# A decay chain and a normalisation with operands in PSUM, and a later place for six weight-column reductions

## The chip, the cores and the metric

One core of a Trainium2 chip runs the whole layer. Five engines work beside each other: TensorE (PE, matrix products), VectorE (DVE), ScalarE (ACT), GpSimd (POOL) and SyncE (SP, which issues nearly all DMAs). The metric is the device time of one execution in microseconds; lower is better.

## The reference

One layer of a decoder trunk on `x` of 1024 tokens by 1024 features, float32. A conditioning vector gives six modulation vectors of 1024 values (`silu(c) @ w_ada + b_ada`). The first half of the layer:

```python
h = rms_norm(x, norm1_w) * (1.0 + scale1) + shift1
proj = h @ w_in            # gq gk gv gz (512 each), ga gb (8 each), sq (512), sk sv (128 each)
q_g, k_g = l2_norm(silu(conv(gq))), l2_norm(silu(conv(gk)))
beta = sigmoid(gb)
g = -exp(a_log) * softplus(ga + dt_bias)       # log-decay, one number per token and head
o_g = gated_delta_rule_chunked(q_g, k_g, v_g, g, beta)   # chunks of 64 tokens, G = cumsum(g) in a chunk
o_s = sliding_window_attention(sq, sk, sv)     # window 128
x = x + gate1 * (concat(o_g, o_s) @ w_out)
```

The second half is a SwiGLU feed-forward network on a second modulated norm. It is not touched here.

## The kernel before

Features lie on the 128 partitions, tokens on the free axis, in two halves of 512 tokens. Each float32 product is made of three: a high part `hi`, rounded by ACT, and a low part `lo = value - hi` stand for both operands, and `mm3` (L223) issues hi*hi, hi*lo, lo*hi. One "step" is one such triple for one block of 128 features; a projection unit of 128 columns by 512 tokens is eight steps into one PSUM bank.

The text of the kernel is traced by a framework. PE runs its instructions in the order in which they are written. On the other engines, and in the DMA queue of SP, a planner sets a fixed order from its own simulated times and from priorities: `tc.high_priority()` raises what is traced in it, and `tc.issue_after(ins)` places what is traced in it behind `ins`, but only those instructions that run on the engine of `ins`. All engines then run their queues in order and wait for semaphores.

Four PSUM banks (tags `u`, `sw`, two buffers each) serve the projection units, four more (tags `q0`, `q1`, and two of `qq`) everything else; `sm()` hands out these in turn.

The work around the change, in order:

- A start stage (to about 66 us) normalises the first half of the tokens and runs the first four projection units and three units of the small projection (`skv`: keys and values of the window attention, `ga`, `gb`).
- The second half of norm 1: `norm1_gen(1, 3)` squares, sums, takes the root, and `rstd_row` (L295) spreads it over the partitions by four transposes into the bank `rowps`, which ACT copies to `row` in SBUF. `modulate1` (L352) then makes `hi` and `lo` for each of the eight feature blocks: even blocks by a product on DVE (L343), ACT's rounding (L344), and a low part on DVE (L345); odd blocks by a product on POOL (L346), two passes on ACT (L348, L349), and a low part on DVE (L350).
- The adaptation columns: each of 48 columns needs the row products of a 128x1024 weight tile, loaded by SP (L260), with a broadcast of the conditioning vector. DVE does it in one instruction (L266), POOL in two products and ACT in a sum (L269, L270). `ada_pair` gives one column to POOL and one to DVE. Columns 0 to 15 are in the start stage, 16 to 31 (eight pairs) are queued behind the norm, 32 to 43 (six pairs) come later, 44 to 47 still later.
- `fill(n)` issues `n` steps of the dense stream: the units gk2, gq2 (both halves), skv 4 to 7, and then, from step 67, the units gk0, gq0, gk1, gq1 (second half), gk3, gq3 and so on. Each finished unit is evacuated by a causal convolution: ACT's first tap (L376), three DVE taps from PSUM (L378), three short DVE corrections from `tails` (L384), and ACT's Silu.
- `token_gen` (L656): the decay chain. For 128x64 numbers (8 heads by 8 blocks of 128 tokens) it makes beta and g with 21 small DVE instructions and three exponentials on ACT (L661 to L681), all on the SBUF tile `tsc`; then the sums over a chunk on PE (`psg`, L686) with DVE's copies of them (L688, L689) and ACT's exponentials (L690 to L692); then transposes (`pst`, L697) and stores to the DRAM tile R, which every pair reads back.
- `PAIRS` (L898): for each of four pairs of heads three visits (`pair_stats`, `pair_rows`, `pair_products`), each between two `fill` calls of the list `VISITS_A`. Then a triangular `solve` (L827) on DVE, the scan over chunks, the window attention, the output projection and the feed-forward network.

In the kernel before, 66 steps of the dense stream stand ahead of the chain, 22 between the chain and its sums, 4 between sums and transposes, and 4 more before the first pair's visit.

Of the kernel before, what the change touches and what calls it, by code (L numbers as in the profile page):

```python
# [12 lines left out]
AF = mybir.ActivationFunctionType  # L13
# [4 lines left out]
P = 128  # L18
# [4 lines left out]
H = 8  # L23
# [31 lines left out]
def tile_hybrid_layer(  # L55
# [61 lines left out]
    def r(ap):  # L117
        return ap.bitcast(F32R)
# [35 lines left out]
    def xs(k, hf):  # L154
        return xt[k // 2, hf][:, k % 2]
# [39 lines left out]
    def pool_tt(out, in0, in1, op, n):  # L195

        m = out.shape[1] // n
        for i in range(n):
            s_ = slice(i * m, (i + 1) * m)
            done["pool"] = pool.tensor_tensor(out=out[:, s_], in0=in0[:, s_], in1=in1[:, s_], op=op)  # L200
# [94 lines left out]
    def rstd_row(rs, name, q=None):  # L295

        pr = sm(f"rowps_{name}", q)
        for i in range(4):
            pe.transpose(out=pr[:, i * P:(i + 1) * P], in_=bc(rs[:, i:i + 1], (P, P)), identity=ident)
        row = t2(f"row_{name}")  # L300
        done["row"] = act.activation(out=row, in_=pr, func=AF.Copy)
        return row

# [35 lines left out]

    def modulate(hi, lo, out, x, row, a, sh, eng):  # L340

        if eng is dve:
            done["dve"] = dve.scalar_tensor_tensor(out=out, in0=x, scalar=a, in1=row, op0=ALU.mult, op1=ALU.mult)  # L343
            act.activation(out=r(hi), in_=out, func=AF.Identity, bias=sh)  # L344
            done["lo"] = dve.scalar_tensor_tensor(out=r(lo), in0=out, scalar=sh, in1=hi, op0=ALU.add, op1=ALU.subtract)  # L345
        else:  # L346
            pool_tt(out, x, row, ALU.mult, 1)
            act.activation(out=r(hi), in_=out, func=AF.Identity, scale=a, bias=sh)  # L348
            act.activation(out=out, in_=out, func=AF.Identity, scale=a, bias=sh)  # L349
            done["lo"] = dve.tensor_tensor(out=r(lo), in0=out, in1=hi, op=ALU.subtract)  # L350

    def modulate1(k, hf, row):  # L352
        hi, lo = h_hl(hf)(k)
        modulate(hi, lo, xs(k, hf), xs(k, hf), row, a1[:, k:k + 1], modc[:, k:k + 1], dve if (k % 2 == 0 if hf else k in (0, 1, 2, 7)) else pool)

# [275 lines left out]
    next(n1)  # L631
    for k in range(KT):
        modulate1(k, 1, rows[1])
    h_done = done["pool"], done["lo"]
    for u in (2, 3):
        EVAC[START[u][0]](START[u][1], 0, ps_u[u])
    for i in range(3):
        skv_out(ps_s[i], i)

# [16 lines left out]
    def token_gen():  # L656
        tsc = t4("tsc", (P, 16, H, NB), tag="a")
        xa, eb, ab, ue, ss_, s2, lp, gt = (tsc[:, n] for n in range(8))
        ealog = tsc[:, 8, :, 0]
# [11 lines left out]
        dve.tensor_scalar(out=ss_, in0=ue, scalar1=2.0, scalar2=None, op0=ALU.add)  # L671
        dve.reciprocal(out=ss_, in_=ss_)
        dve.tensor_tensor(out=ss_, in0=ss_, in1=ue, op=ALU.mult)
        dve.tensor_tensor(out=s2, in0=ss_, in1=ss_, op=ALU.mult)
        dve.tensor_scalar(out=lp, in0=s2, scalar1=1.0 / 17.0, scalar2=None, op0=ALU.mult)
        for n in (15, 13, 11, 9, 7, 5, 3):
            dve.scalar_tensor_tensor(out=lp, in0=lp, scalar=1.0 / n, in1=s2, op0=ALU.add, op1=ALU.mult)
        dve.scalar_tensor_tensor(out=lp, in0=lp, scalar=1.0, in1=ss_, op0=ALU.add, op1=ALU.mult)
        dve.tensor_scalar(out=xa, in0=xa, scalar1=0.0, scalar2=None, op0=ALU.max)
        dve.scalar_tensor_tensor(out=lp, in0=lp, scalar=2.0, in1=xa, op0=ALU.mult, op1=ALU.add)  # L680
        done["token"] = dve.scalar_tensor_tensor(out=gt, in0=lp, scalar=-1.0, in1=bc(ealog.unsqueeze(2), (P, H, NB)),  # L681
                                                 op0=ALU.mult, op1=ALU.mult)
# [5 lines left out]
        dve.tensor_copy(out=gst[:, 2], in_=psg[:, 0:64])  # L688
        dve.tensor_tensor(out=ed.rearrange("p h b -> p (h b)"), in0=psg[:, 64:128], in1=gst[:, 2], op=ALU.subtract)  # L689
        act.activation(out=gst[:, 3], in_=psg[:, 64:128], func=AF.Exp)  # L690
        act.activation(out=gst[:, 1], in_=gst[:, 2], func=AF.Exp)
        act.activation(out=ed, in_=ed, func=AF.Exp)  # L692
        dve.tensor_scalar(out=gst[:, 0], in0=beta.rearrange("p h b -> p (h b)"), scalar1=-1.0, scalar2=None, op0=ALU.mult)
        yield
# [224 lines left out]
    for i in range(11):  # L919
        fill(VISITS_A[0])  # L920
        if i < ADA_FIRST:
            with tc.issue_after(h_done[0].ins), tc.issue_after(h_done[1].ins):
                ada_pair()
    with tc.high_priority():
        next(token)

    with tc.issue_after(done["token"].ins):
        for i in range(11, 14):
            fill(VISITS_A[0])
            for _ in range(3):  # L930
                if ada_next[0] < 44:
                    ada_pair()
    p0, p1, p2, p3 = PAIRS
    for n, visit in zip(VISITS_A[1:], (token, token, p2, p0, p2, p0, p2, p1, p0, keys, p1, p3, keys, p1, keys, p3, p3)):
        fill(n)
        with tc.high_priority():
            next(visit)
# [770 lines left out]
```

## Time and profile before

| | |
|---|---|
| median of 3 runs | 1285.83 us (1284.82 to 1289.03) |
| profiled execution, its own time | 1288.89 us |
| its span, first to last instruction | 1287.2 us |
| PE busy | 1192.2 us (93%) |
| DVE busy | 855.9 us (66%) |
| ACT busy | 534.5 us (42%) |
| POOL busy | 525.9 us (41%) |
| mean granted PE clock | 0.959 of full speed |

Busy times are of one profiled execution. A busy time holds any slowing that the instruction met while it ran, so an instruction of one form can have two very different lengths. Idle time of an engine is listed with what ended it.

### The profile page before, as it was taken

The page shows a single profiled execution, that of the slowest core. Times are in us where ns is not written, and L with a number is a line of the kernel's source. Part 1 is how long each engine was busy: PE and PEld are TensorE (multiplying, and loading weights), DVE is VectorE, ACT ScalarE, POOL GpSimd, SP SyncE. Part 2 cuts the span into 40 slices and gives each one's busy share as a digit, 9 for nine tenths or more (in the row PEclk, how much of TensorE's full clock was granted, in tenths as well). Part 3 has the DMA queues.
Part 4 walks back from the last instruction along what each step waited for, and adds up shares of the span by engine and source line. Part 5 has one row for each costly group of instructions (what it writes and reads, how often), then busy time and mean ns, then how long its engine had stood idle before and what let it go on. Part 6 is the DMA issues. An engine that isn't in the chain of part 4 may idle for free.

```text
span 1287.2 us, 18639 instructions
## 1 busy us (share of the span) xinstructions
PE 1192.2 (93%) x6710; PEld 980.0 (76%) x6710; DVE 855.9 (66%) x1487; ACT 534.5 (42%) x973; POOL 525.9 (41%) x434
## 2 busy tenths in 40 slices
PE   6869497997999899999997989999999999999998
PEld 5758376885788677788876868888888888788887
DVE  6988989879323577545656469777888786665420
ACT  4374455522334587434554442222222243544430
POOL 4677455647536344365544420000000025366440
PEclk8899799997999799999999989999999999999999
DMA  8638369594749756343486885565455678776651
GB/s 331 229 99 310 115 126 241 169 259 130 208 147 213 105 98 154 126 147 134 170 263 219 289 271 192 185 223 172 157 174 176 238 248 307 273 268 202 212 164 41
DMA packets 173548, 250.61 MB, mean 195 GB/s; under 512 B 41360, under 2 KB 107152, under 8 KB 171920
## 3 DMA queue, kind: packets, MB, share of 16 engines
q1 hardware_dynamic: 163856, 241.03, 58.6%
q0 software_dynamic: 9600, 8.39, 4.4%
q8 instruction: 53, 0.87, 0.3%
q14 instruction: 39, 0.32, 0.1%
HBM read 182.89 MB, written 66.45 MB: 194 GB/s over the span
## 4 chain that ended last, share of the span: by engine, by line
PE 61%; DVE 19%; DMA 10%; ACT 5%; issue 2%; SPq 2%; POOL 1%; DVEq 0%; ACTq 0%; POOLq 0%
PE ps_S L1404 7%; PE ps_S L1402 7%; PE ps_S L1403 7%; PE ps_P L1403 5%; PE ps_P L1402 5%; PE ps_P L1404 5%; PE ps_o L225 2%; PE ps_o L227 2%; PE ps_o L226 2%; PE ps_c L1402 2%; PE ps_c L1403 2%; PE ps_c L1404 2%; DVE ada L458 1%; DMA rP<-in_wdown_dram 1%; DMA sd<-in_wdown_dram 1%
## 5 line engine op out<-in xcount | busy, mean ns | idle before, releaser
L200 POOL TENSOR_TENSOR wP<-rP,wP 128x512 fp32r<-128x512 f32 (+1 forms) x84 | 110.1, 1324 | 394.7 <-ACT wP L204 393.3
L1403 PE MATMUL ps_P<-t,wP 128*128 128x512 f32 x308 | 120.5, 391 | 1.1 <-DVE t L208 1.1
L1402 PE MATMUL ps_P<-t,wP 128*128 128x512 f32 x308 | 120.7, 392 | 0.1
L1404 PE MATMUL ps_P<-t,wP 128*128 128x512 f32 x308 | 120.4, 391 | 0.0
L204 ACT ACTIVATE wP<-rP 128x512 fp32r<-128x512 f32 (+1 forms) x84 | 47.4, 588 | 76.9 <-PE ps_P L1404 31.7
L1402 PE MATMUL ps_c<-B,w 128*128 128x512 f32 x176 | 70.3, 400 | 9.1 <-ACT X L1446 9.0
L1403 PE MATMUL ps_c<-B,w 128*128 128x512 f32 x176 | 69.5, 395 | 0.0
L1404 PE MATMUL ps_c<-B,w 128*128 128x512 f32 x176 | 69.5, 395 | 0.0
L1403 PEld LDWEIGHTS ps_P<-t,wP 128*128 128x128 f32 x308 | 57.8, 188 | 14.5 <-DVE t L208 2.2
L1402 PEld LDWEIGHTS ps_P<-t,wP 128*128 128x128 f32 x308 | 57.8, 188 | 12.9 <-ACT t L204 0.5
L1404 PEld LDWEIGHTS ps_P<-t,wP 128*128 128x128 f32 x308 | 57.8, 188 | 12.7
L200 POOL TENSOR_TENSOR ada<-ada,cb 128x512 f32<-128x512 f32 x34 | 50.5, 1517 | 19.1 <-DMA w_gz_0r<-in_wmain_dram 10.7
L1512 ACT ACTIVATE sg<-sg 128x512 f32<-128x512 f32 x33 | 20.9, 632 | 88.0 <-DVE sg L1508 88.0
L225 PE MATMUL ps_o<-mix,w_o 128*128 128x512 f32 x128 | 51.8, 405 | 0.0
L227 PE MATMUL ps_o<-mix,w_o 128*128 128x512 f32 x128 | 50.0, 391 | 0.0
L226 PE MATMUL ps_o<-mix,w_o 128*128 128x512 f32 x128 | 50.0, 391 | 0.0
L1589 DVE SCALAR_TENSOR_TENSOR x1r<-ps_P,modc,x1r 128x512 f32<-128x512 f32 x16 | 11.9, 747 | 54.6 <-PE ps_P L1404 54.6
L1402 PEld LDWEIGHTS ps_c<-B,w 128*128 128x128 f32 x176 | 33.7, 192 | 18.1 <-ACT X L1446 11.2
L1402 PE MATMUL ps_S<-T,wS2h 128*128 128x512 f32 x88 | 35.6, 404 | 3.9 <-ACT wS2h L204 3.9
L1404 PEld LDWEIGHTS ps_c<-B,w 128*128 128x128 f32 x176 | 33.6, 191 | 7.2
L1403 PEld LDWEIGHTS ps_c<-B,w 128*128 128x128 f32 x176 | 33.6, 191 | 6.8
L1404 PE MATMUL ps_S<-T,wS2l 128*128 128x512 f32 x88 | 35.6, 404 | 1.0 <-DVE wS2l L208 1.0
(500 smaller groups left out, 3644.0 us busy)
## 6 DMA issues: line engine op xcount, KB each, us to landing
ada<-in_ada_dram SPq DMA_DIRECT2D x48, 512.0 KB, 4.8
AD<-ops SPq DMA_DIRECT2D x11, 1536.0 KB, 6.1
w<-in_wgate_dram SPq DMA_DIRECT2D x44, 256.0 KB, 3.1
w<-in_wup_dram SPq DMA_DIRECT2D x44, 256.0 KB, 3.8
rP<-SD SPq DMA_DIRECT2D x16, 704.0 KB, 5.5
sd<-in_wdown_dram SPq DMA_DIRECT2D x20, 512.0 KB, 5.6
SD<-sd SPq DMA_DIRECT2D x20, 512.0 KB, 3.6
rP<-in_wdown_dram SPq DMA_DIRECT2D x12, 704.0 KB, 5.7
```

Source lines behind the costliest of these rows:

```text
L200: done["pool"] = pool.tensor_tensor(out=out[:, s_], in0=in0[:, s_], in1=in1[:, s_], op=op)
L204: act.activation(out=r(hi), in_=src, func=AF.Copy)
L225: pe.matmul(out, lhsT=r(lhs[0]), rhs=r(rhs[0]), start=first, stop=False)
L226: pe.matmul(out, lhsT=r(lhs[0]), rhs=r(rhs[1]), start=False, stop=False)
L227: pe.matmul(out, lhsT=r(lhs[1]), rhs=r(rhs[0]), start=False, stop=last)
L458: queue[eng] = getattr(eng, fn)(**kw)
L1402: pe.matmul(ps, lhsT=r(wh), rhs=r(xh), start=first and i == 0, stop=False, **kw)
L1403: pe.matmul(ps, lhsT=r(wh), rhs=r(xl), start=False, stop=False, **kw)
L1404: pe.matmul(ps, lhsT=r(wl), rhs=r(xh), start=False, stop=i == n - 1, **kw)
L1512: act.activation(out=out, in_=out, func=AF.Silu)
L1589: dve.scalar_tensor_tensor(out=x, in0=src, scalar=g2(dt), in1=x, op0=ALU.mult, op1=ALU.add)
```

## The change

- Norm 1, second half: `modulate1` stands alone. On even blocks DVE reads the root's row from the PSUM bank `rowps` itself (`ps_row`) and writes its product to a PSUM bank `xm`, from which ACT and DVE read; on odd blocks the low part moves from DVE to POOL. The eight calls run at raised priority, and the evacuations of the three first `skv` units, whose banks the `xm` tiles take over, are traced ahead of them.
- Decay chain: `xa`, `eb`, `ue`, `ss_`, `s2`, `lq`, `st` lie in one PSUM bank `chn`, and `ab`, `sc`, `lp`, `gt` stay in SBUF. One DVE instruction is added (a second copy of the quotient, `st`). The product of beta with -1 moves from DVE to ACT.
- Order: 66 steps still stand ahead of the chain, then 16 (22 before) ahead of its sums, 6 (4 before) ahead of the transposes, 7 (4 before) ahead of the first pair: 95 in all for 96. `done["token"]` is set once more, by the DVE instruction that makes `ed` from the sums, and the six late pairs of columns are traced behind that one; so their DVE instructions queue behind the sums, not behind the chain.

```diff
 def rstd_row
+        done["rowps"] = pr
...
+    def modulate1(k, row, ps_row):
+        hi, lo = h_hl(1)(k)
+        x, a, sh = xs(k, 1), a1[:, k:k + 1], modc[:, k:k + 1]
+        if k % 2 == 0:
+            out = sm(f"xm{k}", k // 2 % 3)
+            done["dve"] = dve.scalar_tensor_tensor(out=out, in0=x, scalar=a, in1=ps_row, op0=ALU.mult, op1=ALU.mult)
             act.activation(out=r(hi), in_=out, func=AF.Identity, bias=sh)
             done["lo"] = dve.scalar_tensor_tensor(out=r(lo), in0=out, scalar=sh, in1=hi, op0=ALU.add, op1=ALU.subtract)
         else:
-            pool_tt(out, x, row, ALU.mult, 1)
...
-            done["lo"] = dve.tensor_tensor(out=r(lo), in0=out, in1=hi, op=ALU.subtract)
+            pool_tt(x, x, row, ALU.mult, 1)
+            act.activation(out=r(hi), in_=x, func=AF.Identity, scale=a, bias=sh)
+            act.activation(out=x, in_=x, func=AF.Identity, scale=a, bias=sh)
+            pool_tt(r(lo), x, hi, ALU.subtract, 1)
...
-    for k in range(KT):
-        modulate1(k, 1, rows[1])
+    for i in range(3):
+        skv_out(ps_s[i], i)
+    with tc.high_priority():
+        for k in range(KT):
+            modulate1(k, rows[1], done["rowps"])
...
-        xa, eb, ab, ue, ss_, s2, lp, gt = (tsc[:, n] for n in range(8))
+        chn = sm("chn").rearrange("p (n h b) -> p n h b", n=8, h=H)
+        xa, eb, ue, ss_, s2, lq, st = (chn[:, n] for n in range(7))
+        ab, sc, lp, gt = (tsc[:, n] for n in range(4))
...
-        dve.reciprocal(out=ss_, in_=ss_)
-        dve.tensor_tensor(out=ss_, in0=ss_, in1=ue, op=ALU.mult)
-        dve.tensor_tensor(out=s2, in0=ss_, in1=ss_, op=ALU.mult)
+        dve.reciprocal(out=sc, in_=ss_)
+        dve.tensor_tensor(out=st, in0=sc, in1=ue, op=ALU.mult)
+        dve.tensor_tensor(out=sc, in0=sc, in1=ue, op=ALU.mult)
+        dve.tensor_tensor(out=s2, in0=sc, in1=st, op=ALU.mult)
...
-        dve.tensor_tensor(out=ed.rearrange("p h b -> p (h b)"), in0=psg[:, 64:128], in1=gst[:, 2], op=ALU.subtract)
+        done["token"] = dve.tensor_tensor(out=ed.rearrange("p h b -> p (h b)"), in0=psg[:, 64:128], in1=gst[:, 2],
+                                          op=ALU.subtract)
...
-        dve.tensor_scalar(out=gst[:, 0], in0=beta.rearrange("p h b -> p (h b)"), scalar1=-1.0, scalar2=None, op0=ALU.mult)
+        act.activation(out=gst[:, 0], in_=beta.rearrange("p h b -> p (h b)"), func=AF.Copy, scale=-1.0)
...
     for i in range(11):
-        fill(VISITS_A[0])
+        with tc.issue_after(h_done[0].ins):
+            fill(VISITS_A[0])
...
     with tc.issue_after(done["token"].ins):
-        for i in range(11, 14):
-            fill(VISITS_A[0])
-            for _ in range(3):
+        fill(16)
+    with tc.high_priority():
+        next(token)
+
+    with tc.issue_after(done["token"].ins):
+        for _ in range(3):
+            fill(2)
+            for _ in range(2):
                 if ada_next[0] < 44:
                     ada_pair()
...
-    for n, visit in zip(VISITS_A[1:], (token, token, p2, p0, ...
+    for n, visit in zip((0, 7) + VISITS_A[4:], (token, p2, p0, ...
```

`h_done[0]` is the last POOL instruction of the norm: before, the last product of an odd block; after, the last low part of one. The columns 16 to 31 queue behind it on POOL, and behind `h_done[1]` on DVE.

## Rows read from the trace of the kernel before

**Rows 1.** The page: the chain that ended last, share of the span by engine.
```profile
PE 61%; DVE 19%; DMA 10%; ACT 5%; issue 2%; SPq 2%; POOL 1%; DVEq 0%; ACTq 0%; POOLq 0%
```

**Rows 2.** Busy us by stretch: PE, PEld, DVE, ACT, POOL; clock, DMA share, GB/s.
```profile
75.00:165.00 90.00, 64.86 (x307) 53.82 (x306) 78.37 (x111) 47.85 (x90) 61.59 (x42) 0.87 0.49 171
165.00:262.00 97.00, 88.08 (x637) 73.20 (x636) 87.49 (x162) 50.90 (x76) 61.47 (x49) 0.96 0.73 187
```

**Rows 3.** Waits of PE, 75 to 165 us: total us, times, longest.
```profile
PE pst L697 <- ACT gst L691: 10.4, 1, 10.4
PE ps_gk L225 <- ACT kq L400: 7.6, 1, 7.6
PE ps_gk L227 <- POOL w_gk L200: 3.6, 1, 3.6
PE ps_gk L225 <- ACT w_gk L204: 1.6, 1, 1.6
PE pst L697 <- ACT gst L690: 1.2, 1, 1.2
PE psg L686 <- DVE tsc L681: 0.8, 1, 0.8
```

**Rows 4.** Single lines, 60 to 345 us: ns minimum/median/maximum, first and last start.
```profile
L343 DVE SCALAR_TENSOR_TENSOR xt<-xt,a,row_n x4: 767/1778/1782, 77.2 to 81.3; 128x512 f32<-128x512 f32 x4
...
L345 DVE SCALAR_TENSOR_TENSOR h<-xt,modc,h x4: 1091/1414/1784, 84.3 to 90.0; 128x512 fp32r<-128x512 f32 x4
...
L350 DVE TENSOR_TENSOR h<-xt,h x4: 678/1264/1744, 91.0 to 97.1; 128x512 fp32r<-128x512 f32 x4
...
L378 DVE SCALAR_TENSOR_TENSOR qt<-ps_gq,sml,qt x24: 730/736/748, 83.0 to 207.7; 128x511 f32<-128x511 f32 x8, 128x510 f32<-128x510 f32 x8, 128x509 f32<-128x509 f32 x8
```

**Rows 5.** Groups of DVE by form, 116 to 143 us: busy us, mean ns, idle.
```profile
L677 DVE SCALAR_TENSOR_TENSOR tsc<-tsc 128x64 f32<-128x64 f32 x5 | 6.0, 1206 | 0.2
L266 DVE CUSTOM_DVE_ANT_0 ada<-ada,cb 128x1024 f32<-128x1024 f32 x3 | 5.7, 1937 | 0.0
```

**Rows 6.** The same for 143.7 to 160 us.
```profile
L266 DVE CUSTOM_DVE_ANT_0 ada<-ada,cb 128x1024 f32<-128x1024 f32 x6 | 7.2, 1216 | 0.0
```

**Rows 7.** DVE in order of time: start us, length us, line.
```profile
126.12 0.28 DVE L661 TENSOR_TENSOR tsc<-abt,rv 128x64 f32<-128x64 f32 x1 [3.47 <-ACT abt L365]
...
133.86 0.55 DVE L672 RECIPROCAL tsc<-tsc 128x64 f32<-128x64 f32 x1
...
144.83 0.23 DVE L681 SCALAR_TENSOR_TENSOR tsc<-tsc 128x64 f32<-128x64 f32 x1
...
156.57 0.21 DVE L688 COPY gst<-psg 128x64 f32<-128x64 f32 x1
```

**Rows 8.** ACT in order of time.
```profile
126.44 1.28 ACT L663 ACT_TABLE_LOAD   x1
```

**Rows 9.** Groups of POOL, 75 to 165 us.
```profile
L200 POOL TENSOR_TENSOR ada<-ada,cb 128x512 f32<-128x512 f32 x28 | 42.4, 1549 | 8.4 <-DMA ada<-in_ada_dram 8.4
...
L200 POOL TENSOR_TENSOR w_gq<-w_gq_1r,w_gq 128x512 fp32r<-128x512 f32 x4 | 5.1, 1286 | 0.0
```

**Rows 10.** POOL in order of time.
```profile
79.04 6.41 POOL L200 TENSOR_TENSOR xt<-xt,row_n 128x512 f32<-128x512 f32 x4
...
136.16 2.50 POOL L200 TENSOR_TENSOR w_gk<-w_gk_1r,w_gk 128x512 fp32r<-128x512 f32 x2
```

**Rows 11.** PE in order of time.
```profile
95.74 0.77 PE L225 MATMUL ps_gk<-h,w_gk2h 128*128 128x512 f32 x1 [7.58 <-ACT kq L400]
...
108.42 0.28 PE L225 MATMUL ps_skv<-wk_hi,h 128*128 128x272 f32 x1
...
120.53 0.40 PE L225 MATMUL ps_gk<-h,w_gk 128*128 128x512 f32 x1
...
159.00 0.48 PE L697 MATMUL pst<-ident,gst 128*128 128x128 f32 x1 [10.40 <-ACT gst L691]
```

**Rows 12.** Waits of SP's DMA queue, 40 to 165 us.
```profile
SPq L260 <- DVE modc L266: 29.7, 9, 15.0
```

More of the change, by code (lines that the diff above doesn't have):

```diff
@@ L338, in norm1_gen @@
         yield
-    def modulate(hi, lo, out, x, row, a, sh, eng):
-        if eng is dve:
-            done["dve"] = dve.scalar_tensor_tensor(out=out, in0=x, scalar=a, in1=row, op0=ALU.mult, op1=ALU.mult)
+    def modulate1(k, row, ps_row):
[4 more added lines that the diff above has]
+            done["dve"] = dve.scalar_tensor_tensor(out=out, in0=x, scalar=a, in1=ps_row, op0=ALU.mult, op1=ALU.mult)
             act.activation(out=r(hi), in_=out, func=AF.Identity, bias=sh)
@@ L346, in modulate @@
         else:
-            pool_tt(out, x, row, ALU.mult, 1)
-            act.activation(out=r(hi), in_=out, func=AF.Identity, scale=a, bias=sh)
-            act.activation(out=out, in_=out, func=AF.Identity, scale=a, bias=sh)
-            done["lo"] = dve.tensor_tensor(out=r(lo), in0=out, in1=hi, op=ALU.subtract)
-    def modulate1(k, hf, row):
-        hi, lo = h_hl(hf)(k)
-        modulate(hi, lo, xs(k, hf), xs(k, hf), row, a1[:, k:k + 1], modc[:, k:k + 1], dve if (k % 2 == 0 if hf else k in (0, 1, 2, 7)) else pool)
+            pool_tt(x, x, row, ALU.mult, 1)
+            act.activation(out=r(hi), in_=x, func=AF.Identity, scale=a, bias=sh)
+            act.activation(out=x, in_=x, func=AF.Identity, scale=a, bias=sh)
+            pool_tt(r(lo), x, hi, ALU.subtract, 1)
     ktok, vs, abt = None, None, cp.tile([P, NB, 16], F32, name="abt")
@@ L636, in tile_hybrid_layer @@
         EVAC[START[u][0]](START[u][1], 0, ps_u[u])
-    for i in range(3):
-        skv_out(ps_s[i], i)
     def chain(*gens):
@@ L677, in token_gen @@
             dve.scalar_tensor_tensor(out=lp, in0=lp, scalar=1.0 / n, in1=s2, op0=ALU.add, op1=ALU.mult)
-        dve.scalar_tensor_tensor(out=lp, in0=lp, scalar=1.0, in1=ss_, op0=ALU.add, op1=ALU.mult)
+        dve.scalar_tensor_tensor(out=lp, in0=lp, scalar=1.0, in1=st, op0=ALU.add, op1=ALU.mult)
         dve.tensor_scalar(out=xa, in0=xa, scalar1=0.0, scalar2=None, op0=ALU.max)
-        dve.scalar_tensor_tensor(out=lp, in0=lp, scalar=2.0, in1=xa, op0=ALU.mult, op1=ALU.add)
-        done["token"] = dve.scalar_tensor_tensor(out=gt, in0=lp, scalar=-1.0, in1=bc(ealog.unsqueeze(2), (P, H, NB)),
+        dve.scalar_tensor_tensor(out=lq, in0=lp, scalar=2.0, in1=xa, op0=ALU.mult, op1=ALU.add)
+        done["token"] = dve.scalar_tensor_tensor(out=gt, in0=lq, scalar=-1.0, in1=bc(ealog.unsqueeze(2), (P, H, NB)),
                                                  op0=ALU.mult, op1=ALU.mult)
@@ L933, in tile_hybrid_layer @@
     p0, p1, p2, p3 = PAIRS
-    for n, visit in zip(VISITS_A[1:], (token, token, p2, p0, p2, p0, p2, p1, p0, keys, p1, p3, keys, p1, keys, p3, p3)):
+    for n, visit in zip((0, 7) + VISITS_A[4:], (token, p2, p0, p2, p0, p2, p1, p0, keys, p1, p3, keys, p1, keys, p3, p3)):
         fill(n)
```

## The prediction

> **What bounds the kernel now.** I read the chain that ended last first: PE holds 61% of it, DVE 19% [rows 1]. So the end is PE's work plus the times in which PE stands still. PE runs in the written order, and what it does after 165 us stays as it was; a stall that goes before then moves the rest forward. I therefore read busy time by stretch next. From 75 to 165 us PE is busy for 64.9 of 90 us, DVE for 78.4; from 165 to 262 us PE for 88.1 of 97 and DVE for 87.5 [rows 2]. The first stretch, the one that the change touches, has 25.1 us of idle PE; the second has little left on either engine.
>
> The list of PE's waits names these 25 us [rows 3]: 7.6 for the bank of a query unit, which DVE's convolution gives back late; 1.6 and 3.6 for the split weights of gk1 from ACT and POOL; 0.8 for the decay chain; 10.4 and 1.2 for the sums of the chain on their way to the transposes. The reader should see that all but the 5.2 for the weights end in DVE.
>
> Then the question is why DVE is late. The single lines answer it [rows 4]: the convolution L378, one tensor from PSUM and one from SBUF, takes 730 to 748 ns in all 24 cases; L343 and L345, of the same size and operation but with both tensors in SBUF, take up to 1.78 us. In the decay chain the five L677 that run while POOL is busy take 1206 ns [rows 5], and L681, of the same form, when POOL's queue has run dry, takes 0.23 [rows 7]. So a DVE instruction with two SBUF tensors waits for POOL, one with a tensor in PSUM does not. The chain also has one-source instructions from SBUF; the trace shows none of these from PSUM beside POOL, only the 64-column copy L688 at 0.21 [rows 7], with POOL idle.
>
> **The change part by part.**
>
> *Norm 1.* Removed: L343 and L345 at SBUF speed and four L350. I take the medians, 1.78, 1.41 and 1.26, four of each: 17.8 us; added, eight at 0.74: 5.9. DVE saves 11.9, of which about 9.5 (all but two L350) stand ahead of the query convolution that frees the bank. PE stood still until 95.74 after 7.58 of waiting [rows 11], so from 88.2; the bank would be free at some 86. The raised priority puts the convolutions behind the products, which costs little where DVE has this room. Bounds: nothing gained if the planner moves them to the end of the low parts; all 7.6 otherwise. I take 7.1. PE also ran its first matmul behind this stall at 0.77 where 0.39 is usual [rows 11]; for the stretch of matmuls at the lower clock level I take 1.3, between 0 and 3.
>
> POOL gets four low parts at 1.29 (as the weight splits [rows 9]), and its four products, 6.41 us from 79.04 on [rows 10], fall to 1.29 each, since DVE no longer holds it up. Its column products so start at 79.0 + 8 x 1.29 = 89.3, 3.9 us later. PE, ready at 88.2, needs the first new low part in its second step, at 88.9, and the last in its eighth, at 93; by POOL's order (four products, four low parts) the first is there at 85.5 and the last at 89.3. That is hidden, with 3.4 us to spare.
>
> *Decay chain.* Before: from 126.12 to 145.06, 18.9 us [rows 7]. After, DVE has 22 instructions: one with two SBUF tensors (0.28), two reciprocals at 0.55, 19 at 0.23, together 5.8. To this comes ACT's table load, 1.28 [rows 8], and three hand-overs to ACT and back, 1.2 in all (an estimate, from DVE's start at 126.12 and ACT's at 126.44). Sum 8.3, saved 10.6. Bounds: 7.1, with hand-overs hidden, and 18.9, if PSUM operands help one-source instructions nothing and the others pay for it. I take the value near the rows of the right form, L378 and L688.
>
> The rows show DVE free to work while ACT loads its table from 126.44 to 127.72 [rows 8]; none shows the two at work on one bank. The Trainium skill, PSUM — Partial Sum Buffer, section "PSUM bank collisions raise a hardware error", says that two engines may not use a bank in the same partition in the same cycle. By this rule the exponential's write to the chain's bank and DVE's reads of it must follow each other, and the two instructions that make `ab` would come behind the table load: estimated 0.5 us more. By the rows alone they would cost nothing. No run here shows it yet; the sum leaves it out.
>
> *Where the chain starts and ends.* PE's last skv unit ended at 120.5 [rows 11], the chain began 5.6 later, since ACT, in order, was behind a column sum that waited for POOL. With the bank's 7.1 and the clock's 1.3 PE is there at 112. The 32 skv steps of 272 columns took 12.1 us (108.42 to 120.53 [rows 11]), 0.38 each, so by columns a step of 512 is 0.71; the 16 ahead of the sums take 11.4, and PE asks for the sums at 123. The chain, begun between 112 and 118, ends between 120 and 126. I leave PE 1.0 of waiting there, for 0.8 before.
>
> *The sums.* The sums could be read from some 145.6 on, right behind the chain, but DVE copied them at 156.57 [rows 7]: six column reductions, 7.2 us [rows 6], and two convolutions stood in its queue. After, the reductions queue behind the sums. Convolutions of the two finished units may still go first, at most 2 x 2.9 us (three taps at 0.74, three corrections at 0.23). From copy to transposes ACT needs another table load, 1.3, and two exponentials, about 2.5 in all; PE has six steps, 4.3 us, in between. I leave no wait, so 11.6 saved, with 5.0 as lower bound.
>
> *Weights of gk1.* PE now asks for them at 123 us; before, POOL had split them at 138.7 [rows 10], behind 26 of the 28 column products. POOL's queue from 89.3: 26 products at 1.29 to 1.55, two splits of 2.6, and none or all of the 8.4 of DMA waits [rows 9] give 128 to 143; if the planner puts the split ahead of the late columns, it is ready at once. I take 130, near the quick end: the loads behind those waits came when DVE's low parts gave back their buffers, and these now end 7 us earlier. A wait of 7.0 for 5.2 before: 1.8 lost. The bounds are 5.2 gained and 13 lost, but with a wait this long the sums are hidden behind it. This is where the change turns one wait into another.
>
> *Sum for PE to 165 us.* 7.1 + 1.3 - 0.2 + 11.6 - 1.8 = 18.0 gained. DVE allows it: it saves 11.9 and 12.5 (18.2 us busy in the chain and its copy of beta, against 5.8) of 78.4, and would be busy 54 of 72 us.
>
> *What goes downstream.* The 95th instead of the 96th step ahead of the first pair moves one step behind it, no work added: 0. The product of beta on ACT: 0.3 under the fills. The bank that the chain takes shifts the turn of the four small banks by one; each still comes back after four: 0. SP's queue: before, column loads waited there for up to 15.0 us at a time for reductions on DVE [rows 12]; the next weights and the stores to R stand behind them. The reductions now come right behind `ed`, ahead of the transposes, so I cost it at 0. The six reductions, 7.2 us, now run close to the first pair's work and beside a busy POOL, where one takes 1.94 [rows 5], 11.6 in all; DVE's 9.5 idle us from 165 to 262 [rows 2] take them: 0, at worst all of it lost.
>
> Profiled execution: 1288.9 - 18.0 = 1270.9 us. It is 3.1 above the median of the three runs; against that median, 1285.8 - 18.0 = 1267.8, told as 1268.
>
> **The rivals.**
>
> *Given back in the pairs.* The six reductions and the two held convolutions fall into the pairs' stage, and DVE, 90% busy there, becomes its limit: 11.6 plus 2 of the second convolution lost, 4.4 gained: 1281. For it: DVE's 87.5 of 97. Against: the visits have raised priority, the columns not, and DVE arrives there with less work behind it. Chance 0.12.
>
> *PSUM does not help.* One-source instructions and PSUM writes are held up by POOL all the same. Then the chain still takes about 19, PE asks for the sums at 123 plus 4 lost in norm 1 and waits 14 us; the sums' 11.6, four L350 (4.9) remain as gains, and no wait for weights: about 1275. Against it: 24 even L378. Chance 0.05.
>
> *No change.* The start of the solve is set by transfers and by DVE's own chain, whatever PE gains: the chain holds 10% DMA [rows 1]. 1286. Against it: DVE, too, gains more than PE. Chance 0.07.
>
> *Slower: SP's queue.* If the planner puts the late reductions not right behind `ed` but behind the first pair's statistics, the column loads that wait for their buffers stand in SP's queue ahead of the stores to R and of the weights of gk3. From a delay of about 18 us on, this costs more than the rest gains. With 25, one wait of 15.0 [rows 12] and ten more, the time is 1285.8 - 18 + 25 = 1293. For it: SP waits 29.7 us for these reductions already. Against it: the text puts the reductions behind one DVE instruction that is done before the transposes can start. Chance 0.07.
>
> **How the numbers follow.** The forecast, 1257 to 1276, has 0.69: at the lower end all 25.1 us of idle PE and 3 of clock go, at the upper POOL is late by 13 and hides the sums' gain in part. The range, for 8 in 10, is 1257 to 1282: it takes in the second rival and half of the first. A measurement can tell 0.3%, 3.9 us, from no change, so faster means under 1282: 0.69 + 0.05 + 0.08 = 0.82; the same 0.10, from the rest of the first rival and the third; slower 0.08.
>
> **What would show it.** The product and low part of even blocks at 0.65 to 0.8 us each, whatever POOL does; no PE wait for the query bank; the chain in 7 to 10 us, and its 64-column instructions near 0.23 beside a busy POOL; the copy of the sums within 6 us of the sums; a wait of PE for gk1's weights as the largest one left before the first pair; the first pair's transposes some 18 us earlier, and every later stage by as much. The forecast fails if the chain stays over 14 us, if the first pair gains under 8 us, or if the pairs' stage grows by more than 5.

## The result

Four runs of the changed kernel took 1269.28 to 1273.70 us, median 1271.47, beside 1285.48 for the kernel before on the same chip: ratio 0.9886, interval 0.9857 to 0.9914. It is faster by 14.0 us; 18.0 were forecast. The time is 3.5 above the forecast (1268) and inside the range. A second comparison, six runs on another occasion, gave 1272.35 and 0.9885 [0.9848, 0.9923]. Each ratio here and below is taken over the fast executions of its comparison, so it is not exactly the quotient of the medians beside it.

The profiled execution took 1269.28 us. Its stretches, columns as in [rows 2]:

```profile
75.00:165.00 90.00, 78.32 (x393) 65.90 (x392) 72.18 (x130) 55.65 (x105) 79.18 (x54) 0.94 0.66 203
165.00:262.00 97.00, 87.67 (x625) 73.13 (x626) 82.40 (x159) 45.70 (x65) 60.04 (x50) 0.93 0.74 195
```

In the stretch that was changed PE is busy for 78.3 us, 13.5 more than in [rows 2]. PE's waits there, 25.2 us in [rows 3], are two:

```profile
PE psg L690 <- DVE tsc L685: 6.1, 1, 6.1
PE ps_gq L227 <- POOL w_gq L200: 0.8, 1, 0.8
```

The wait for the query bank, the waits for gk1's weights and the wait of the transposes are gone. Ahead of the first pair only the chain is waited for; the 0.8 for gq comes later, at 159.74. The lines of norm 1 (ns minimum/median/maximum) answer to L343 and L345 of [rows 4]:

```profile
L347 DVE SCALAR_TENSOR_TENSOR xm<-xt,a,rowps_n x4: 748/750/754, 77.7 to 84.3; 128x512 f32<-128x512 f32 x4
```

and POOL in order of time answers to [rows 10]:

```profile
77.73 5.06 POOL L200 TENSOR_TENSOR xt<-xt,row_n 128x512 f32<-128x512 f32 x4 [0.25 <-ACT row_n L301]
83.14 2.71 POOL L200 TENSOR_TENSOR h<-xt,h 128x512 fp32r<-128x512 f32 x2 [0.35 <-ACT xt L353]
86.53 3.57 POOL L200 TENSOR_TENSOR h<-xt,h 128x512 fp32r<-128x512 f32 x2 [0.68 <-ACT xt L353]
90.06 3.53 POOL L200 TENSOR_TENSOR ada<-ada,cb 128x512 f32<-128x512 f32 x2
```

Every DVE product takes 0.75, whatever POOL does. The chain, the sums and what follows them on DVE, for [rows 7]:

```profile
119.42 0.27 DVE L664 TENSOR_TENSOR chn<-abt,rv 128x64 f32<-128x64 f32 x1 [4.72 <-ACT abt L365]
122.40 0.23 DVE L667 TENSOR_SCALAR tsc<-chn 128x64 f32<-128x64 f32 x1 [2.71 <-ACT chn L666]
...
125.99 1.75 DVE L681 SCALAR_TENSOR_TENSOR tsc<-tsc,chn 128x64 f32<-128x64 f32 x7
...
128.64 0.23 DVE L685 SCALAR_TENSOR_TENSOR tsc<-chn,tsc 128x64 f32<-128x64 f32 x1
...
131.29 0.21 DVE L692 COPY gst<-psg 128x64 f32<-128x64 f32 x1
...
132.52 0.21 DVE L693 TENSOR_TENSOR ed<-psg,gst 128x64 f32<-128x64 f32 x1
...
143.42 1.14 DVE L705 COPY drow<-tsc 64x2 f32<-64x2 f32 x1
...
158.48 2.28 DVE L768 TENSOR_TENSOR ee<-ee,cmask 128x1024 f32<-128x1024 f32 x1 [4.54 <-POOL ee L200]
...
167.05 0.19 DVE L191 SCALAR_TENSOR_TENSOR rn<-rsq_g 128x32 f32<-128x32 f32 x1
```

From 119.42 to 128.87 the chain takes 9.45 us, 18.94 before. Its seven L681 take 1.75 together, beside POOL at work without a pause:

```profile
113.56 10.99 POOL L200 TENSOR_TENSOR ada<-ada,cb 128x512 f32<-128x512 f32 x8
```

**Where the time went afterwards.** I follow marks on PE that both kernels have: the first transposes of the sums (`pst`), of the first pair (`pst_k`), the first `psr_k` (transposes of `wide_k`, which ACT spreads from the inverse norms `rn` of the first pair), and the first matmul `pk` of the scan. DVE makes `rn` by an inverse root with Newton steps; `ee` holds the decays between tokens, loaded from R. After:

```profile
136.37 0.38 PE L702 MATMUL pst<-ident,gst 128*128 128x128 f32 x2
...
141.39 1.04 PE L733 MATMUL pst_k<-ident,kn 128*128 128x128 f32 x8
...
168.78 1.97 PE L750 MATMUL psr_k<-ident,wide_k 128*128 128x128 f32 x8 [8.54 <-ACT wide_k L746]
...
335.23 1.16 PE L1084 MATMUL pk<-S,kvq 128*128 128x128 f32 x8
```

Before, the last three (the first is in [rows 11]), and DVE's `rn`:

```profile
165.18 1.03 PE L728 MATMUL pst_k<-ident,kn 128*128 128x128 f32 x8
...
182.32 1.03 PE L745 MATMUL psr_k<-ident,wide_k 128*128 128x128 f32 x8
...
349.98 1.16 PE L1074 MATMUL pk<-S,kvq 128*128 128x128 f32 x8
...
176.91 0.59 DVE L191 SCALAR_TENSOR_TENSOR rn<-rsq_g 128x32 f32<-128x32 f32 x1
```

The lead is 159.00 - 136.37 = 22.6 us at the sums, 23.8 at the first pair, 13.5 at `psr_k`, 14.8 at `pk`. So more was gained up to 165 us than forecast (18.0), and 10.3 were lost inside the first pair. SP's queue shows where that begins:

```profile
138.75 0.80 SPq L707 DMA_DIRECT2D R<-tsc  x2
...
144.59 0.52 SPq L708 DMA_DIRECT2D Rd<-drow  x1
145.20 7.16 SPq L762 DMA_DIRECT2D ee<-R  x4
```

The store to R comes 22.8 us earlier than before (161.55). The next store, Rd, waits for the two-column copy `drow`, which stands on DVE behind the column reductions until 143.42; the loads of `ee` stand behind Rd and come 19.4 us earlier (before 164.60).

The rest of the loss shows in DVE's order. Before, all Newton steps of the first pair's `rn` stood ahead of the product of `ee` (L763 at 178.49), and `rn` was ready at 176.91. After, the planner has that product (now L768) ahead of the last Newton steps: DVE stands still for 4.54 us until POOL delivers `ee`, which waits for its load, and `rn` is made at 167.05. Its lead is 9.9, and PE's `psr_k` waits 8.5 for it. Further on the lead falls to 7.7 where `psr_s` waits 13.6 us (6.1 before), and is back at 13.5 with the unit after it. No run changed DVE's order alone, so its share is read from the trace, not shown.

### The profile page after: what moved, and what is told of

Read it like the earlier page. It is cut to its first block, busy times and chain, and to the rows that moved or that the text cites. A ratio compares the mean times of both kernels' runs of the same rounds, so it can differ in the third digit from the quotient of the medians.

```text
span 1267.6 us, 18646 instructions
## 1 busy us (share of the span) xinstructions
PE 1182.0 (93%) x6710; PEld 971.4 (77%) x6710; DVE 829.1 (65%) x1483; ACT 536.4 (42%) x974; POOL 539.6 (43%) x438
## 4 chain that ended last, share of the span: by engine, by line
PE 65%; DVE 14%; DMA 9%; ACT 5%; POOL 3%; issue 2%; SPq 1%; DVEq 0%; ACTq 0%; POOLq 0%
PE ps_S L1414 8%; PE ps_S L1412 8%; PE ps_S L1413 8%; PE ps_P L1414 6%; PE ps_P L1412 6%; PE ps_P L1413 6%; PE ps_o L225 2%; PE ps_o L227 2%; PE ps_o L226 2%; DVE ada L458 2%; DMA ada<-in_ada_dram 2%; POOL ada L200 1%; DMA sd<-in_wdown_dram 1%; PE ptr L1091 1%; PE ps_gz L225 1%
## 5 line engine op out<-in xcount | busy, mean ns | idle before, releaser
L200 POOL TENSOR_TENSOR ada<-ada,cb 128x512 f32<-128x512 f32 x34 | 58.7, 1762 | 10.6 <-DMA ada<-in_ada_dram 10.6
L1599 DVE SCALAR_TENSOR_TENSOR x1r<-ps_P,modc,x1r 128x512 f32<-128x512 f32 x16 | 11.9, 748 | 54.3 <-PE ps_P L1414 54.3
L204 ACT ACTIVATE wS2h<-w 128x1024 fp32r<-128x1024 f32 x11 | 11.7, 1066 | 58.8 <-PE ps_S L1413 26.5
```

The source lines that it names most:

```text
L204: act.activation(out=r(hi), in_=src, func=AF.Copy)
L1599: dve.scalar_tensor_tensor(out=x, in0=src, scalar=g2(dt), in1=x, op0=ALU.mult, op1=ALU.add)
```

## The experiments

The prediction put one gain on each part of the change, and none on how they meet. So the three parts were run in all combinations; "norm" is modulate1, "chain" the decays in PSUM, "order" the late columns behind the sums. Beta's product is on ACT in all of them but norm alone. The numbers are median us and the ratio to the kernel before, measured in the same comparison:

| norm | chain | order | label | median | ratio [95%] | `pk` at |
|---|---|---|---|---|---|---|
| x | | | e1_norm | 1279.05 | 0.9935 [0.9911, 0.9958] | 342.4 |
| | x | | e2_chain | 1288.92 | 1.0020 [0.9990, 1.0049] | 353.3 |
| | | x | e3_order | 1279.16 | 0.9958 [0.9928, 0.9987] | 339.8 |
| x | x | | e6_old_order | 1289.49 | 0.9988 [0.9953, 1.0023] | 351.0 |
| x | | x | e5_chain_sbuf | 1280.05 | 0.9925 [0.9895, 0.9955] | 337.6 |
| | x | x | e10_chain_order | 1278.19 | 0.9907 [0.9877, 0.9937] | 338.0 |
| x | x | x | e11_changed_again | 1272.35 | 0.9885 [0.9848, 0.9923] | 336.3 |

From `pk` to the end the profiled executions took 932 to 940 us in all kernels (944 in e2), in no order of the change, so I count that part as not moved. The changed kernel's 932.4, for 937.2 before, is at the short end: 4.8 of its profiled execution's gain lie there.

**Norm 1 alone.** Of the diff, modulate1 and the three lines around it:

```diff
-            done["dve"] = dve.scalar_tensor_tensor(out=out, in0=x, scalar=a, in1=row, op0=ALU.mult, op1=ALU.mult)
+            done["dve"] = dve.scalar_tensor_tensor(out=out, in0=x, scalar=a, in1=ps_row, op0=ALU.mult, op1=ALU.mult)
...
-            done["lo"] = dve.tensor_tensor(out=r(lo), in0=out, in1=hi, op=ALU.subtract)
+            pool_tt(r(lo), x, hi, ALU.subtract, 1)
```

> The norm part alone (row and product in PSUM, low parts of odd blocks on POOL, raised priority), chain and order as before. Theory A (PE's stalls ahead of the first pair are removed one by one, each by its own part): the 7.6 us for the query bank go, the chain still takes about 19 us and the sums still wait about 11 us behind the column reductions; 5 to 8 us faster, 1277 to 1280. Theory B (the order of the columns and sums makes the gain, PSUM operands only empty DVE where it has room): PE comes to the weights and the chain earlier and waits there instead; under 3 us faster, 1283 or more.

1279.05 us, 8.8 below the kernel before. PE's waits from 75 to 165 us:

```profile
PE pst L698 <- ACT gst L692: 10.7, 1, 10.7
PE ps_gk L225 <- ACT w_gk L204: 3.7, 1, 3.7
PE ps_gk L227 <- POOL w_gk L200: 3.1, 1, 3.1
PE psg L687 <- DVE tsc L682: 1.8, 1, 1.8
```

The bank's 7.6 are gone, the others stay (19.3 us for 17.6 before), and `pk` comes 7.6 earlier. This term of the sum (7.1) is right.

**Chain alone.**

```diff
-        xa, eb, ab, ue, ss_, s2, lp, gt = (tsc[:, n] for n in range(8))
+        chn = sm("chn").rearrange("p (n h b) -> p n h b", n=8, h=H)
+        xa, eb, ue, ss_, s2, lq, st = (chn[:, n] for n in range(7))
+        ab, sc, lp, gt = (tsc[:, n] for n in range(4))
```

> The chain alone in PSUM, with beta's product on ACT; norm and order as before. Theory A: the chain falls from 18.9 to 8 to 10 us; PE is held by gk1's weights until about 144 all the same, but the six column reductions start 9 us earlier and the copy of the sums with them, so the wait at the transposes falls from 11.6 to about 3: 6 to 9 us faster, 1277 to 1280. Theory B: under 3 us faster. If PSUM operands do not help beside a busy POOL, the chain stays over 15 us.

1288.92 us, no gain, although the chain took 9.44 us. The expectation of a gain failed: PE still waits 11.2 us at the transposes, 11.6 before. The profiled execution, 1299.44, was the slowest of ten.

**Order alone** (of the diff, the place of the sums; beta's product moves to ACT too):

```diff
...
     with tc.issue_after(done["token"].ins):
-        for i in range(11, 14):
-            fill(VISITS_A[0])
-            for _ in range(3):
+        fill(16)
+    with tc.high_priority():
+        next(token)
+
+    with tc.issue_after(done["token"].ins):
+        for _ in range(3):
+            fill(2)
+            for _ in range(2):
...
```

> The order alone (16, 6 and 7 steps, reductions behind the sums, beta's product on ACT), norm and chain in SBUF as before. Theory A: the chain still ends at about 144; PE stands at the sums for 6 to 9 us, but the wait at the transposes (11.6) goes; the first pair's statistics come 5 to 9 us earlier, of which the pair then loses as much as in the changed kernel: 0 to 6 us faster, 1280 to 1286. Theory B: 8 to 14 us faster, 1272 to 1278.

1279.16 us, ratio 0.9958: 5.4 us by the ratio, within Theory A's 0 to 6, while the median lies between the two theories. With the old chain (18.58 us) PE waits for it:

```profile
PE psg L686 <- DVE tsc L681: 12.7, 1, 12.7
PE ps_gk L225 <- ACT kq L400: 7.5, 1, 7.5
```

So the order turns the wait for the sums, in part, into a wait for the chain. By the ratios the short chain is worth nothing without the order (e2, e6), and the order 0.4% with the long chain but 1.0 to 1.1% with the short one (e10 against e2, the changed kernel against e6).

**Chain in SBUF, the rest changed** (the changed kernel without chain):

```diff
-        chn = sm("chn").rearrange("p (n h b) -> p n h b", n=8, h=H)
-        xa, eb, ue, ss_, s2, lq, st = (chn[:, n] for n in range(7))
-        ab, sc, lp, gt = (tsc[:, n] for n in range(4))
+        xa, eb, ab, ue, ss_, s2, lp, gt = (tsc[:, n] for n in range(8))
...
```

> The changed kernel with the decay chain back in SBUF (norm and order stay). Theory A (the parts work only together: with the new order PE stands at the sums until the chain ends, so the chain's length is on the path): the chain starts near 119 and takes 18.6 to 18.9 instead of 9.4, PE waits about 15 us at the sums instead of 6.1, the first pair's statistics come 8 to 10 us later than in the changed kernel; 5 to 9 us slower than it, 1277 to 1281. Theory B (PSUM in the chain is worth nothing, as in the run with the chain alone, 0.999 to 1.005 of before): 1270 to 1273.

1280.05 us; the chain took 16.61 us and PE waited 13.4 for it. Beside the whole change (0.9885) the chain is worth some 0.4%; the intervals overlap, so the longer wait for the chain, 13.4 for 6.1, is shown and the time not by itself.

**Old order, the rest changed:**

```diff
...
     with tc.issue_after(done["token"].ins):
-        fill(16)
-    with tc.high_priority():
-        next(token)
-
-    with tc.issue_after(done["token"].ins):
-        for _ in range(3):
-            fill(2)
-            for _ in range(2):
+        for i in range(11, 14):
+            fill(VISITS_A[0])
+            for _ in range(3):
...
```

> The changed kernel with the old order (22 and 4 steps, late columns behind the chain; norm and chain stay in PSUM). Theory A: the chain ends at about 129, but the six reductions and two convolutions run ahead of the copy of the sums, which comes at about 145; PE waits 5 to 9 us at the transposes; the first pair's statistics come 10 to 13 us earlier than before instead of 23.8, the pair loses little; 1274 to 1279. Theory B (order is cosmetic once DVE has room): 1270 to 1273.

1289.49 us: the whole gain gone, and 0.5% by the ratios, about 7 us, above norm alone, which I had not expected. The chain ends at 129.80, 9.2 us earlier than in e1, but the store to R comes at 153.67 for 154.41 there. DVE copies the sums at 145.38 (written from 137.16 on) and makes `ed` at 149.18, behind reductions and convolutions, and on ACT, in order of time, this breaks the exponentials apart:

```profile
143.17 1.28 ACT L392 ACT_TABLE_LOAD   x1 [4.67 <-DVE kn L384]
...
146.63 1.28 ACT L696 ACT_TABLE_LOAD   x1
...
149.24 1.28 ACT L400 ACT_TABLE_LOAD   x1
...
151.18 1.28 ACT L695 ACT_TABLE_LOAD   x1
...
153.66 1.28 ACT L392 ACT_TABLE_LOAD   x1
```

The exponentials of the sums (L695, L696) fall between the activations of the convolutions (L392, L400): five table loads, 6.4 us, where e1 has three. e2 shows the same five, from 149.19 on. In the changed kernel the sums follow the chain so closely that the three exponentials run from 131.53 to 133.13 with the table that the chain loaded at 120.79; the next load is at 135.48. Then, from an equal start, e6 loses to e1 in the first pair, by DVE's order again:

```profile
170.79 2.29 DVE L768 TENSOR_TENSOR ee<-ee,cmask 128x1024 f32<-128x1024 f32 x1 [6.47 <-POOL ee L200]
...
179.16 0.18 DVE L191 SCALAR_TENSOR_TENSOR rn<-rsq_g 128x32 f32<-128x32 f32 x1
```

In e1 `rn` stands ahead of this product and is ready at 169.10, 10 us earlier. A later unit adds more: `psr_s` waits up to 15.4 us in e6 and 15.7 in e2, 7.0 in e1, so that e6 reaches `pk` 8.6 later than e1; but this wait differs as much between two profiles of one kernel (see the low parts on DVE, below). No run changed the table loads or DVE's order by themselves, so that they make the whole difference is read from the traces, not shown.

**Chain and order, norm as before:**

```diff
-            done["dve"] = dve.scalar_tensor_tensor(out=out, in0=x, scalar=a, in1=ps_row, op0=ALU.mult, op1=ALU.mult)
+            done["dve"] = dve.scalar_tensor_tensor(out=out, in0=x, scalar=a, in1=row, op0=ALU.mult, op1=ALU.mult)
```

> The chain in PSUM and the new order of the columns, without the change of norm 1 (its row is copied to SBUF and the low parts are on DVE, as before). Norm 1 alone was worth 8.8 us, the order alone 5.4, the chain alone nothing, norm 1 and chain nothing, norm 1 and order 9.7, all three 14. Theory A (norm 1's bank wait lies on the path whatever the rest does): the wait for the bank of kq is back at 7 us, and the time is 7 to 10 us above the changed kernel, a ratio of 0.993 to 0.996. Rival (the parts stand in one line, and PE waits for the chain's sums anyway, so that 7 us earlier columns only lengthen that wait): within 3 us of the changed kernel, PE's wait for psg under 1 us.

1278.19 us (runs from 1265.59 to 1290.57), 5.8 above the changed kernel's median in the same comparison; by the ratios it is 0.2%, about 3 us, and the intervals overlap. What norm adds to the other two parts is therefore not shown in time. PE waits from 75 to 165 us:

```profile
PE ps_gk L225 <- DVE tails L381: 6.5, 1, 6.5
PE psg L689 <- DVE tsc L684: 4.0, 1, 4.0
```

The bank's wait is back at 6.5, while that for the chain falls from 6.1 to 4.0: with all parts together norm's gain is partly spent in waiting for the chain, as the rival said. The difference by the ratios is the rival's too; the 4.0 are not the under 1 that it named.

**`drow` on ACT.** Against the changed kernel:

```diff
-        dve.tensor_copy(out=drow[64:128], in_=grow[64:128, 1, 0:128:64])
+        act.activation(out=drow[64:128], in_=grow[64:128, 1, 0:128:64], func=AF.Copy)
```

> The changed kernel with one instruction moved: the 64x2 copy drow by ACT, not by DVE. In the changed kernel this copy starts at 143.42 on DVE, behind five column reductions, and SP's queue holds its store ahead of the loads of ee, which the first pair's statistics need; the 23.8 us by which the first pair's transposes are early fall to 13.5 at its rows. Theory C (the loss is that queue): loads of ee start about 139 instead of 145, rows of the first pair 4 to 6 us earlier, 2 to 5 us faster than the changed kernel, 1266 to 1269. Theory D (the loss is DVE's own backlog of reductions and convolutions): the rows move by under 2 us, 1270 to 1272.

1268.21 us, 0.9869 [0.9821, 0.9917]. SP's queue and PE:

```profile
138.52 0.53 SPq L708 DMA_DIRECT2D Rd<-drow  x1
...
140.69 8.48 SPq L762 DMA_DIRECT2D ee<-R  x4
...
163.07 1.97 PE L750 MATMUL psr_k<-ident,wide_k 128*128 128x128 f32 x8 [5.15 <-ACT wide_k L746]
```

The loads of `ee` come 4.5 us earlier, `rn` at 161.54 instead of 167.05, `psr_k` 5.7 earlier. So the place of `drow` cost this. The median is only 3.3 below the changed kernel's, and the two were not compared side by side: the gain in time stays unproven, the cause in the trace is shown. Of the lead lost in the first pair 5.7 us are left, for 10.3. `pk` comes at 323.6, 11.6 earlier than in the changed kernel, but this profile also has a `psr_s` wait of 4.7 for 13.6, and the next kernel shows both lengths.

**Low parts of the odd blocks on DVE.** Against the changed kernel:

```diff
-            pool_tt(r(lo), x, hi, ALU.subtract, 1)
+            done["lo"] = dve.tensor_tensor(out=r(lo), in0=x, in1=hi, op=ALU.subtract)
```

> The changed kernel with the four low parts of odd blocks back on DVE (all else stays). Theory E (POOL is the engine that now sets the start of the chain, through the column sums on ACT: four low parts cost it 5 us): POOL's columns start about 84 instead of 90, the chain 2 to 4 us earlier, DVE has 3 us more work of its own and the query bank comes at most 2 us late; within 3 us of the changed kernel, 1268 to 1274. Theory F (DVE sets it): the bank wait of 3 to 7 us is back and the chain starts no earlier; 3 to 7 us slower, 1274 to 1278.

1265.55 us, 0.9813 [0.9772, 0.9854], better than the changed kernel. It and the changed kernel were then run again side by side:

> The changed kernel itself, unaltered, beside the three others on the same chip. Its first comparison gave a ratio of 0.9886, but the kernel before has run between 1278 and 1300 us in the later comparisons, so the small differences between variants need one common base. All theories expect a ratio of 0.985 to 0.991 again; outside that, differences of 3 us between variants that were not compared together carry no weight.

> The variant with the odd blocks' low parts of norm 1 on DVE, unaltered, beside the changed kernel. Theory E (the low parts on POOL cost time, since POOL's bias additions stand behind them): 4 to 8 us faster than the changed kernel, a ratio near 0.981. Rival (the first comparison's difference of 0.007 came from the chip, since both traces have nearly the same lead at the decays' sums, 23.4 and 22.6 us): within 2 us of the changed kernel.

1272.35 us (six runs, 1266.26 to 1278.13) for the changed kernel, 1265.90 (four runs, 1264.21 to 1268.69) for this variant: 6.5 us faster, for 5.9 between the first two medians; ratios to the kernel before 0.9885 [0.9848, 0.9923] and 0.9833 [0.9803, 0.9863]. The two intervals overlap a little, but both comparisons agree. POOL, SP's queue and PE in e7:

```profile
82.77 5.96 POOL L200 TENSOR_TENSOR ada<-ada,cb 128x512 f32<-128x512 f32 x4
...
143.60 4.28 SPq L762 DMA_DIRECT2D ee<-R  x4
147.92 1.59 SPq L708 DMA_DIRECT2D Rd<-drow  x1
...
165.26 1.97 PE L750 MATMUL psr_k<-ident,wide_k 128*128 128x128 f32 x8 [6.49 <-ACT wide_k L746]
```

POOL's column products begin at 82.77 instead of 90.06, and no wait for the query bank comes back. At the sums the lead is little better (23.4 us for 22.6); at `psr_k` it is 17.1 for 13.5, 16.8 in the second profile. So the low parts on POOL, which the prediction costed as hidden, cost time later, in the first pair. The trace shows one way: with them on DVE the planner has the loads of `ee` ahead of Rd in SP's queue, not behind it, and DVE's product of `ee` waits 1.02 us for POOL instead of 4.54. Whether that is all of it is not shown. This is the fastest kernel that I have.

The two profiles of this one kernel, e7 and e12, also show how far a mark moves with no edit at all: `psr_s` waits 5.3 us in one and 13.5 in the other, and `pk` comes at 327.2 and 332.6. ACT stands behind a column sum that waits 9.1 and 17.7 us for POOL, and in e12 one product of POOL, where its counterpart in e7 takes 1.4, takes 9.23:

```profile
280.75 9.23 POOL L200 TENSOR_TENSOR ada<-ada,cb 128x512 f32<-128x512 f32 x1
```

Beside it DVE runs the solve without a pause, all operands in SBUF, until 288.86; the product ends 1.1 us later. All profiles fall into two groups here, with 4.7 to 7.0 us of this wait (before, e1, e3, e4, e5, e7, e8) or 13.4 to 15.7 (the changed kernel twice, e2, e6, e9, e10, e12). A difference of 5 us at `pk` between two kernels with one profile each is therefore not shown to come from an edit.

**Both of these together:**

> The variant with the low parts on DVE, and with the two-column copy drow on ACT instead of DVE, so that SP's store and the loads of ee no longer stand behind the column reductions on DVE. Theory C (the place of drow behind the reductions is a price of the moved columns): 3 to 5 us faster than the variant with the low parts on DVE alone, the loads of ee issued at 139 to 141 us instead of 143.6, and PE's waits for wide_k 3 us shorter; ratio 0.977 to 0.979. Rival (the lead at the first pairs is covered by a later wait for the transposed rows of the second pair or by the granted clock in the scan): the loads come earlier, and the time is within 2 us.

1268.91 us, 0.9854 [0.9821, 0.9888]: no gain over the low parts on DVE alone. The loads of `ee` were not earlier (143.80). ACT shows why:

```profile
138.01 1.28 ACT L392 ACT_TABLE_LOAD   x1 [6.44 <-DVE kn L384]
...
139.84 0.37 ACT L703 ACTIVATE tsc<-pst 128x256 f32<-128x256 f32 x1
```

Here the copy that the store to R needs stands on ACT behind an activation that waits 6.44 us for DVE, so R itself comes at 140.23, and `drow` is no longer what is late. The expectation failed on its premise.

**More column sums kept back.** Against e4: ADA_FIRST 4 instead of 8, four pairs of columns behind the chain's last exponential:

```diff
-ADA_FIRST = 8
+ADA_FIRST = 4
...
+    with tc.issue_after(done["ue"].ins):
+        for _ in range(4):
+            ada_pair()
```

> The kernel with drow on ACT, and ACT's column sums of all pairs but the first four queued behind the chain's exponentials, so that the last block of decay inputs is not behind them. Theory G (the 6 to 7 us that PE still waits at the sums come from ACT standing behind column sums that wait for POOL): the chain starts at 112 to 115 instead of 118 to 119, PE waits 0 to 3 us at the sums, 2 to 4 us faster than with drow on ACT alone, 1264 to 1266. Theory H: held back column buffers delay POOL, the loads on SP and with them the stores to R by as much; no gain or slower, 1268 to 1274.

DVE, and PE's waits from 75 to 165 us:

```profile
114.44 1.32 DVE L664 TENSOR_TENSOR chn<-abt,rv 128x64 f32<-128x64 f32 x1
...
PE ps_gk L227 <- POOL w_gk L200: 9.8, 1, 9.8
PE ps_gk L225 <- ACT w_gk L204: 2.1, 1, 2.1
```

The chain starts 5.0 us earlier than in the changed kernel and PE no longer waits for it; but POOL splits gk1's weights at 133.65, behind its columns, and PE waits 11.9 for them. The sums are there 6.3 us earlier (122.62), the transposes 5.7 later (142.07). The median is 1280.05; the profiled execution, at 1269.48, was the fastest of ten, so its trace does not explain the median. The gain that Theory G expected did not come.

## Why the prediction was right, and where not

| Step | Forecast | Measured |
|---|---|---|
| wait for the query bank | 7.1 gained | gone; e1: `pk` 7.6 earlier |
| PE free for the sums | at 123 | 128.92 - 6.12 = 122.8 |
| POOL's columns start | 89.3 | 90.06 |
| chain, length | 8.3 | 9.45 |
| chain, end | 120 to 126 | 128.87 |
| PE's wait for it | 1.0 | 6.1 |
| wait of the transposes | none left | none left |
| weights of gk1 | 7.0 | 0; 0.8 for gq |
| lead at the first pair | 18.0 | 23.8 |
| lost downstream | 0 | 10.3 in the first pair, 1.3 regained up to `pk` |

**Right.** The cause that the whole argument stands on: a DVE instruction that reads one of its operands from PSUM does not wait for POOL. L347 takes 0.75 four times, the chain's 64-column instructions 0.22 to 0.23, those with one source and those that write PSUM too, which [rows 5] and [rows 7] had left open; the rival by which PSUM does not help falls with that. A PSUM target alone does not do it: L664, two SBUF sources into PSUM, took 0.27 us in the changed kernel, but 0.79 in e7 and 1.32 in e8, beside POOL. The reductions came right behind `ed`, as the text had it.

**Chain, 1.2 us too short.** DVE's 22 instructions add up to 5.9 us, as forecast (5.8). The difference lies in the 2.71 us ahead of L667, of which the table load's 1.28 was in the sum. ACT first makes a column sum (119.62 to 120.79), which I had not counted, then loads the table (1.28) and writes `eb` into the chain's bank, and only then does DVE make `ab`. In e5, with the chain in SBUF, the same instruction follows the first one at once (119.54). So the two engines take turns at the bank, which is what the Trainium skill (PSUM — Partial Sum Buffer, section "PSUM bank collisions raise a hardware error") asks for; the trace agrees in every kernel with the chain in PSUM. It is the built program that takes turns: L667 reads `xa`, which is ready, and is released by ACT's write of `eb`; no run shows what the chip would do otherwise. The price is ACT's wait for `ab` ahead of the second exponential, in ACT's order of time:

```profile
122.98 0.23 ACT L669 ACTIVATE chn<-tsc 128x64 f32<-128x64 f32 x1 [0.61 <-DVE tsc L668]
```

0.61 us for the estimated 0.5. The column sum's 1.2 weighs more; together they exceed the 1.2 missed, since the other hand-overs took less than estimated.

**Chain's start, the mis-sized term.** PE ended its last skv unit at 111.9, as I had it (112), but DVE began at 119.42, not between 112 and 118: ACT's copy of that unit stood behind a column sum that waited 6.04 us for POOL. I had seen this very thing [rows 7, 11] and expected it to shrink. It grew, from 5.6 to 7.5 us, since PE is there 8.6 earlier and ACT's copy only 6.7. That POOL's columns start later has little part in it: in e7 they start 7.3 us earlier and the chain 1.4 (118.06), and the second profiles of the two kernels have the chain at the same time (118.81 and 118.82). e8 took the wait away (114.44), and paid it back in weights.

**Weights.** I had them ready at 130, and PE waiting 7.0 for them. POOL begins gk1's split at 129.41, behind 24 column products; PE, held by the chain until 128.92, needs its first half at 130.79, when that is just done. So the wait for the chain covered the wait for the weights: 6.1 and 0, where I had 1.0 and 7.0. e8 shows that the price was real: with the chain 5.0 earlier and 26 products ahead of the split it is 11.9.

**Downstream, the step that failed.** I set it at 0, "at worst all of it lost". The first pair lost 10.3 us, of which 1.3 came back up to `pk`. I had looked at SP's queue for the column loads and at DVE for its load; neither was it. Rd waits for `drow`, which takes 3.4 of the lead of the loads of `ee`; with that undone in e4, 4.6 of the 10.3 are gone. For the rest, DVE's order puts `rn` behind a product that waits for a transfer. That is the rival of transfers that set the pace, in part: the loads of `ee` take 7.2 us (7.8 before), whatever PE gains. By the prediction's own signs one of failure came true, since the stage of the pairs, from `pst_k` to `pk`, grew by 9.0, more than 5, and two of success did not: gk1's weights were not the largest wait left, and the later stages did not keep the first pair's lead. That the total came out near the forecast is luck in this: a lead at the first pair 5.8 larger than summed met this loss of 9.0. Of the 23.8, 19.1 are waits (25.2 less 6.1); the other 4.7 are matmuls at a mean granted clock of 0.94 instead of 0.87, and one step fewer ahead of the pair, which the runs do not tell apart.

**The chances** are not quite consistent: half of the first rival's 0.12 is counted into the range up to 1282, but 0.08 of it into the times under 1282.

## What to carry to other kernels

Price a set of edits by what each leaves waiting, not by adding gains: a chain cut by half was worth nothing until its reader stood next in every queue, and the reordering alone turned much of the wait for the sums into one for the chain. When work moves past others, read the new order of each in-order engine: the smallest instruction that a DMA waits for, an instruction that now waits for a DMA ahead of ready work, and activations whose functions alternate, since each change costs a table load (1.28 us here).

## What the runs showed that I had not expected

Between a PSUM source and a PSUM target DVE is not held up by POOL either: L683, 128x64, took 0.23 us, where the SBUF form of such an instruction took 1.30 us in e1 (L672). POOL, in turn, still pays for DVE's SBUF work: the two gq splits at 109.03 took 4.58 us beside column reductions, against 5.06 for four products at 77.73, beside DVE work that reads PSUM. The 9.23 us of one product in e12 is such a price too.
